# A hybrid decoder layer on one core: the scheduler's order taken from another timing model

## The chip, the cores and the metric

The kernel runs on one core of one Trainium2 chip. The metric is the device time of one execution in microseconds; three runs are timed, and one further execution is profiled.

## The reference

One layer of a decoder is computed for 2048 prompt tokens and for 64 sample tokens (8 sequences of 8), in fp32, with a model width of 1024. Two head groups share one input projection: attention over a sliding window of 128 with learned sinks, and an RWKV-7 recurrence whose state is corrected at each token. Their outputs are put side by side and projected; a gated feed-forward layer with a causal convolution of width 3 follows.

```python
proj = _rms_norm(x, g_pre_mix) @ w_in                 # q, k, v of attention and h of the recurrence
o_attn = attention(rope(q), rope(k), v, sinks)        # 8 heads of 64, 2 kv heads, window 128
def step(S, inp):                                     # the recurrence, 8 heads, S is 64 x 64
    r_t, w_t, k_t, v_t, kk_t, a_t = inp
    sa = jnp.einsum('bhij,bhj->bhi', S, kk_t)
    S = (S * w_t[:, :, None, :] - sa[..., None] * (kk_t * a_t)[:, :, None, :]
         + v_t[..., None] * k_t[:, :, None, :])
    return S, jnp.einsum('bhij,bhj->bhi', S, r_t)
o_rw = (group_norm(ys) + bonus) * g
mix = jnp.concatenate([o_attn, o_rw], axis=-1) @ w_out
x = x + _rms_norm(mix, g_post_mix)
z, u = split(_rms_norm(x, g_pre_ffn) @ w_ffn_in)      # 2 x 2816 columns
x = x + _rms_norm((silu(conv3(z)) * u) @ w_ffn_out, g_post_ffn)
```

## The kernel before

**Dense work.** The tokens are cut into five groups of 448 (the last holds 256 prompt and 64 sample tokens). For each group there are a projection P (20 tasks), an output projection O (8 tasks) and a feed-forward stage in two parts: F0, F2, F4, F6, F8 (60 tasks each) and F1, F3, F5, F7, F9 (6 tasks each). A task is one weight tile `w` of 128 x 1024. It is split into two rounded halves, `wh` by a cast on ACT (L351) and `wl` by a subtraction on DVE (L352), as the activations are (`xhi`, `xlo`), and gives 24 matmuls of 448 columns into one PSUM tile: `xhi`·`wh`, `xlo`·`wh` and `xhi`·`wl` for each of eight k. They show as `gm` or, in the second half of the feed-forward stage, as `pf`, at L182, the line of the helper that records every matmul. The stages follow one another in a list:

```python
order = [P[0], P[1], P[2], O[0], P[3], F[0], O[1], F[1], P[4], F[2], O[2], F[3],
         O[3], F[4], F[5], O[4], F[6], F[7], F[8], F[9]]
```

There are 11280 dense matmuls. P2 begins at the 960th, O0 at the 1440th, P3 at the 1632nd, F0 at the 2112th, P4 at the 3888th, O3 at the 6000th, F4 at the 6336th.

**The mixer.** The prompt is also cut into eight units of 256 tokens. A unit does two blocks of attention (`sc`, a softmax, the transposes `ppt`, then `po`) and the recurrence in four chunks of 64 tokens. The recurrence has a fixed chain of steps: the scores `sc_e` and `sc_o` from `ab`; from them a triangular system `G`; a trip through memory (`dgr`, then `gb`); its inversion by 31 steps of two DVE instructions each, every one on the result of the one ahead; a copy on ACT (L1045) and another trip through memory; small products `pz`; a chain over the chunks (`pc`, `pu`, `pS`); the group norm; and `finish`, with the transposes `pt`, the gate `pg` and the product `fin` (L1221), which goes to memory as `od`.

```python
v.tensor_tensor(out=tm, in0=col, in1=row, op=ALU.mult)                                   # L1041
v.tensor_tensor(out=tt[:nb, w:, 0:w], in0=tt[:nb, w:, 0:w], in1=tm, op=ALU.subtract)     # L1042
...
nc.scalar.copy(out=xx[:nb], in_=tt[:nb].rearrange("q s t -> q t s"))                     # L1045
```

An output projection reads `od` back (`r<-od`, then `xhi` and `xlo`) once the units under its tokens are done: O0 needs units 0 and 1, O1 units up to 3, O2 up to 5, O3 up to 6, O4 all of them. Its k from 0 to 3 are the attention half of the rows, k from 4 to 7 the recurrent half.

**What sets the order.** [...] First the program is written out as one sequence: while the dense stages run, `Flow` puts in the steps of a unit, by a clock that adds up estimated matmul times and by a window for each unit (unit 0 in P1, unit 1 in P2, unit 2 from P3 into F0, units 3 and 4 in F0, 5 and 6 in F2, 7 and the sample tokens in F4). [...] The order that comes out on each engine is fixed, and semaphores are set between the engines. On the chip an engine runs its instructions in that order, so an instruction that isn't ready holds up all that stand behind it on its engine. Nearly all DMAs are issued by SP.

## Time and profile before

| | |
|---|---|
| runs, us | 2903.93, 2908.86, 2918.96 (median 2908.86) |
| the profiled execution, us | 2909.42 |
| its span, us | 2907.6 |
| PE busy | 2772.0 us, 95% |
| DVE busy | 1925.0 us, 66% |
| ACT busy | 1409.1 us, 48% |
| POOL busy | 239.3 us, 8% |
| TensorE granted clock, mean | 0.97 |

The profiled execution took 1.8 us more than its span, and lies 0.6 us above the median. A share of busy time is a mean over stages. An interval of a view gives busy time by engine, and PEclk is the share of full speed that the throttle granted to TensorE.

### The profile page before, as it was taken

How to read it: one execution, taken by the hardware profiler on the slowest of the kernel's cores; microseconds unless marked ns; L12 is line 12 of the kernel's file. 1: busy time of each engine (PE TensorE's matmuls, PEld its weight loads, DVE VectorE, ACT ScalarE, POOL GpSimd, SP SyncE). 2: the span in 40 equal slices, each digit the busy share in tenths (PEclk: the TensorE clock that was granted, in tenths of full speed). 3: DMA queues.
4: the chain of work that ended last, by engine and by line, in shares of the span. 5: the costliest groups of instructions: out<-in, count | busy, mean ns of one | idle time of the engine just before them, and what ended most of it. 6: DMA issues, size and time to landing. Idle time of an engine off the chain costs nothing.

```text
span 2907.6 us, 46258 instructions
## 1 busy us (share of the span) xinstructions
PE 2772.0 (95%) x16993; PEld 2354.7 (81%) x16993; DVE 1925.0 (66%) x3792; ACT 1409.1 (48%) x2628; POOL 239.3 (8%) x519
## 2 busy tenths in 40 slices
PE   8997998989999999998999999899999999999997
PEld 6875776758778789776887898778989999999997
DVE  6884885686756655687665556965764764447666
ACT  6553545546564554454655434455333443334543
POOL 1010010010000000022000010000000001001111
PEclk9997999989999999998999999999999999999998
DMA  6665645746744343565544335664433553335443
GB/s 200 195 201 136 193 142 147 219 127 196 217 143 126 104 148 123 170 198 142 180 134 136 115 108 160 208 196 133 130 115 109 186 182 107 109 105 177 157 150 119
DMA packets 310529, 446.58 MB, mean 154 GB/s; under 512 B 118536, under 2 KB 238952, under 8 KB 310288
## 3 DMA queue, kind: packets, MB, share of 16 engines
q1 hardware_dynamic: 309872, 443.48, 49.5%
q8 instruction: 134, 2.20, 0.3%
q14 instruction: 91, 0.75, 0.1%
q10 hardware_dynamic: 432, 0.16, 0.0%
HBM read 362.19 MB, written 76.97 MB: 151 GB/s over the span
## 4 chain that ended last, share of the span: by engine, by line
PE 75%; DVE 13%; DMA 5%; ACT 3%; issue 3%; SPq 1%; DVEq 0%; ACTq 0%
PE gm L182 46%; PE pf L182 16%; PE pc L182 3%; DVE wl L352 2%; PE po L182 2%; DVE tt L1042 1%; DVE tmp L1041 1%; PE pz L182 1%; PE ppt L186 1%; ACT wh L351 1%; PE sc L182 1%; PE pu L182 1%; DMA w<-in_w_all 1%; PE pS L182 1%; PE sc_e L182 1%
## 5 line engine op out<-in xcount | busy, mean ns | idle before, releaser
L182 PE MATMUL gm<-xhi,wh 128*128 128x448 f32 (+3 forms) x2880 | 1056.1, 369 | 44.2 <-ACT wh L351 18.9
L182 PE MATMUL gm<-xhi,wl 128*128 128x448 f32 (+3 forms) x2880 | 1042.1, 363 | 14.9 <-DVE wl L352 14.6
L182 PE MATMUL gm<-xlo,wh 128*128 128x448 f32 (+3 forms) x2880 | 1039.5, 362 | 4.5 <-DVE xlo L352 4.2
L351 ACT CAST wh<-w 128x1024 fp32r<-128x1024 f32 (+1 forms) x470 | 489.5, 1042 | 720.3 <-PE gm L182 332.8
L352 DVE TENSOR_TENSOR wl<-w,wh 128x1024 fp32r<-128x1024 f32 (+1 forms) x470 | 569.9, 1213 | 381.8 <-ACT wh L351 377.6
L182 PEld LDWEIGHTS gm<-xhi,wh 128*128 128x128 f32 (+2 forms) x2880 | 544.2, 189 | 131.4 <-issue 31.4
L182 PEld LDWEIGHTS gm<-xhi,wl 128*128 128x128 f32 (+2 forms) x2880 | 544.3, 189 | 73.6 <-DVE wl L352 21.0
L182 PEld LDWEIGHTS gm<-xlo,wh 128*128 128x128 f32 (+2 forms) x2880 | 545.3, 189 | 60.3 <-DVE xlo L352 10.6
L182 PE MATMUL pf<-hh,wh 128*128 128x448 f32 (+1 forms) x880 | 317.8, 361 | 3.8 <-DVE acc L908 2.9
L182 PE MATMUL pf<-hl,wh 128*128 128x448 f32 (+1 forms) x880 | 312.5, 355 | 0.6 <-DVE hl L352 0.6
L182 PE MATMUL pf<-hh,wl 128*128 128x448 f32 (+1 forms) x880 | 312.4, 355 | 0.2 <-DVE wl L352 0.2
L881 POOL COPY zcar<-zz 128x2 f32<-128x2 f32 x110 | 74.4, 676 | 1547.6 <-ACT zz L870 1547.6
L908 DVE TENSOR_TENSOR acc<-acc,pf 128x448 f32<-128x448 f32 (+1 forms) x200 | 117.3, 589 | 103.4 <-PE pf L182 102.7
L182 PEld LDWEIGHTS pf<-hh,wh 128*128 128x128 f32 x880 | 165.3, 188 | 23.6 <-DVE acc L908 4.9
L182 PEld LDWEIGHTS pf<-hh,wl 128*128 128x128 f32 x880 | 165.3, 188 | 12.7 <-issue 1.0
L182 PEld LDWEIGHTS pf<-hl,wh 128*128 128x128 f32 x880 | 165.5, 188 | 11.8 <-DVE hl L352 1.0
L877 DVE SCALAR_TENSOR_TENSOR c<-zz,c_cw,c 128x448 f32<-128x448 f32 (+1 forms) x220 | 140.8, 640 | 26.2 <-ACT c L871 24.1
L891 DVE TENSOR_TENSOR c<-c,gm 128x448 f32<-128x448 f32 (+1 forms) x110 | 65.0, 591 | 120.4 <-PE gm L182 94.3
L884 ACT ACTIVATE c<-c 128x448 f32<-128x448 f32 (+1 forms) x110 | 61.2, 557 | 126.5 <-DVE c L877 89.3
L1041 DVE TENSOR_TENSOR tmp<-gb,tt 64x31 f32<-64x31 f32 (+21 forms) x279 | 91.4, 328 | 3.6 <-DMA gb<-dgr 1.0
L1042 DVE TENSOR_TENSOR tt<-tt,tmp 64x31 f32<-64x31 f32 (+21 forms) x279 | 91.9, 329 | 2.8
L351 ACT CAST xhi<-r 128x448 fp32r<-128x448 f32 (+1 forms) x112 | 59.3, 542 | 70.8 <-DMA r<-od 25.8
(272 smaller groups left out, 3115.6 us busy)
## 6 DMA issues: line engine op xcount, KB each, us to landing
w<-in_w SPq DMA_DIRECT2D x220, 512.0 KB
w<-in_w2q SPq DMA_DIRECT2D x100, 512.0 KB
w<-in_w_all SPq DMA_DIRECT2D x90, 512.0 KB
ab<-abd SPq DMA_DIRECT2D x66, 512.0 KB
w<-in_w_out SPq DMA_DIRECT2D x40, 512.0 KB
r<-in_xT SPq DMA_DIRECT2D x56, 224.0 KB
r<-od SPq DMA_DIRECT2D x32, 224.0 KB
x2d<-mx SPq DMA_DIRECT2D x32, 224.0 KB
```

The lines of the kernel that those rows point to most:

```text
L182: return self.te.matmul(out, lhsT, rhs, **kw)
L186: return self.te.transpose(*args)
L351: self.nc.scalar.copy(out=hi, in_=src)
L352: self.nc.vector.tensor_tensor(out=lo, in0=src, in1=hi.bitcast(F32), op=ALU.subtract)
L877: v.scalar_tensor_tensor(out=c[:, :npr], in0=z[:, j:j + npr], scalar=cw(j), in1=c[:, :npr], op0=ALU.mult, op1=ALU.add)
L881: nc.gpsimd.tensor_copy(out=sh.zcar[:, f, :], in_=z[:, npr:npr + 2])
L884: nc.scalar.activation(out=c, in_=c, func=AF.Silu)
L891: v.tensor_tensor(out=c, in0=c, in1=ps, op=ALU.mult)
L908: v.tensor_tensor(out=accs[c], in0=accs[c], in1=ps, op=ALU.add)
L1041: v.tensor_tensor(out=tm, in0=col, in1=row, op=ALU.mult)
L1042: v.tensor_tensor(out=tt[:nb, w:, 0:w], in0=tt[:nb, w:, 0:w], in1=tm, op=ALU.subtract)
```

## The change

The Tile context is opened with another argument: the scheduler's model of the machine is now its timeline model, where it was the clock of the instruction simulator. [...]

```diff
@@ -1652,7 +1652,7 @@
     a = {n: nc.dram_tensor("in_" + n, x.shape, mybir.dt.from_np(x.dtype), kind="ExternalInput").ap() for n, x in arrays.items()}
     for n, shape in out_shapes(seq).items():
         a[n] = nc.dram_tensor("out_" + n, shape, F32, kind="ExternalOutput").ap()
-    with tile.TileContext(nc) as tc:
+    with tile.TileContext(nc, schedule_with_timeline_sim=True) as tc:
         program(tc, nc, a, seq)
     r = run_bass_kernel_spmd(nc, [{"in_" + n: x for n, x in arrays.items()}], core_ids=[0]).results[0]
     return assemble({n: r["out_" + n] for n in out_shapes(seq)}, inputs, seq)
```

The two programs hold the same instructions but for the loads of ACT's function tables (28 before, 24 now); PE has 14441 matmuls in both. On PE an instruction stands on average 18 places from where the program wrote it before, and 131 now; on DVE 9 and 39, on ACT 31 and 45, on SP 16 and 29. The dense matmuls keep their order among themselves, nearly without exception, but the units stand elsewhere among them. The table counts the dense matmuls that stand ahead of a unit's first `sc_e`, first `pz` and last `pg` on PE.

| unit | before | now |
|---|---|---|
| 0 | 643, 848, 1039 | 646, 1082, 1440 |
| 1 | 1078, 1340, 1440 | 1440, 1440, 1476 |
| 2 | 1506, 1812, 2055 | 1479, 1857, 2273 |
| 3 | 2082, 2489, 2616 | 2309, 2719, 3171 |
| 4 | 2649, 2977, 3189 | 3217, 3624, 3925 |
| 5 | 3888, 4392, 4653 | 3953, 4594, 5031 |
| 6 | 4683, 5047, 5319 | 5068, 5479, 5907 |
| 7 | 5973, 6408, 6636 | 5988, 6348, 6718 |
| sample | 6783, 7045, 7181 | 6869, 7173, 7360 |

PE goes from a dense matmul to another kind 1020 times before and 748 times now; behind the start of O0 it is 759 and 609 times.

The first place is the end of P2 on PE. These rows of before run from the last dense matmuls of P2 over a product of its projection (`pb`) and the end of unit 1 (`pt`, `pg`) to two blocks' `sc` of unit 2 and the first matmuls of O0.

```order
L182 MATMUL gm<-xhi,wh 128x448
L182 MATMUL gm<-xlo,wh 128x448
L182 MATMUL gm<-xhi,wl 128x448
L182 MATMUL pb<-b_4964,c_blockones 128x448
L186 MATMUL pt<-c_ident,y 128x128
L182 MATMUL pg<-sg,c_g_up 128x256 x2
L186 MATMUL pt<-c_ident,y 128x128 x7
L182 MATMUL pg<-sg,c_g_up 128x256 x2
L182 MATMUL sc<-kx,q 128x256 x4
L182 MATMUL gm<-xhi,wh 128x448 x2
```

In the change P2's last dense matmul has behind it the end of unit 0 (`pt`, `pg`), and then unit 1 begins with the scores of its attention (`sc`) and of its recurrence (`sc_e`, `sc_o`); no dense matmul of P2 is left.

```order
L186 MATMUL pt<-c_ident,y 128x128 x7
L182 MATMUL pg<-sg,c_g_up 128x256 x2
L182 MATMUL sc<-kx,q 128x256 x4
L182 MATMUL sc_e<-ab 128x128 x4
L182 MATMUL sc_o<-ab 128x128 x4
L182 MATMUL sc<-kx,q 128x256 x4
L182 MATMUL sc_e<-ab 128x128 x4
L182 MATMUL sc_o<-ab 128x128 x4
L182 MATMUL sc_e<-ab 128x128 x4
L182 MATMUL sc_o<-ab 128x128 x4
L186 MATMUL ppt<-c_ident,s 128x128 x8
L182 MATMUL sc_e<-ab 128x128 x4
```

What moved is all of unit 1, from among P2's matmuls to behind them: between P2's last dense matmul and the 37th of O0 there now stand 359 matmuls of other kinds (183 ahead of O0's first, 176 behind its 36th). They are unit 0's end, the last products of P2's projection, and unit 1 from its first `sc` to its last `pg`. O0's 36 are three tasks' k from 0 to 3. On DVE the 62 steps of unit 1's inversion lie in the same place, behind P2's splits. The end of unit 1 in the change, with unit 2's first `sc` and O0's matmuls behind it, reads:

```order
L182 MATMUL pS<-uv,bkt 64x64 x7
L182 MATMUL pc<-uv,G 64x64 x4
L186 MATMUL pt<-c_ident,y 128x128
L182 MATMUL pg<-sg,c_g_up 128x256 x2
L186 MATMUL pt<-c_ident,y 128x128 x7
L182 MATMUL pg<-sg,c_g_up 128x256 x2
L182 MATMUL sc<-kx,q 128x256 x4
L182 MATMUL gm<-xhi,wh 128x448 x3
```

The second place is unit 0's inversion on ACT. In the rows of before, which lie in P1, the copy of its result (`gb<-tt`) stands right ahead of the cast of a weight tile (`wh`).

```order
L722 ACTIVATE e_2412<-L 128x7x64
L725 ACTIVATE e_2384<-L 128x448
L624 COPY qraw<-gm 128x448
L731 ACTIVATE tha<-tha,oka,hka 128x448
L1045 COPY gb<-tt 64x1024
L351 CAST wh<-w 128x1024
L1071 COPY zt<-pz 32x128 x2
```

In the change it stands ten casts of weight tiles later (45 are ahead of it where 35 were).

```order
L351 CAST wh<-w 128x1024
L639 COPY vts<-pvt 112x256 x2
L668 ACTIVATE hm<-gm,omu 128x448
L674 COPY h<-gm 128x448
L668 ACTIVATE hm<-gm,omu 128x448
L674 COPY h<-gm 128x448
L1045 COPY gb<-tt 64x1024
L555 ACTIVATE lo<-lo 32x448
L351 CAST wh<-w 128x8x96
```

What moved is the point in the stream of casts at which ACT takes up the inverse: it leaves P1, and unit 0's `pz` and chain go into P2 with it.

The third place is the start of F4 on PE, where unit 7's `pz` of before lie apart among dense matmuls and transposes (`ppt`) of the attention.

```order
L182 MATMUL pz<-zt,G 32x32
L186 MATMUL ppt<-c_ident,s 128x128 x3
L182 MATMUL pz<-zt,G 32x32 x7
L186 MATMUL ppt<-c_ident,s 128x128
L182 MATMUL gm<-xhi,wh 128x448
L182 MATMUL gm<-xlo,wh 128x448
```

In the change 48 of the 64 lie together behind 27 to 30 dense matmuls of F4.

```order
L182 MATMUL po<-pT,va 64x512
L182 MATMUL pz<-G,zt 32x32 x8
L182 MATMUL pz<-zt,G 32x32 x8
L182 MATMUL pz<-G,zt 32x32 x8
L186 MATMUL ppt<-c_ident,s 128x128 x4
L182 MATMUL pz<-zt,G 32x32 x8
L186 MATMUL ppt<-c_ident,s 128x128 x4
L182 MATMUL po<-pT,va 64x512
L182 MATMUL pz<-G,zt 32x32 x8
L182 MATMUL gm<-xhi,wh 128x448 x3
```

What moved is that the `pz` begin behind 12 dense matmuls of F4 where 72 stood ahead of them before, and come in a lump where they were spread over 42.

## Rows read from the trace of the kernel before

**Rows 1.** The page's head: span, and busy time of each engine.

```profile
span 2907.6 us, 46258 instructions
PE 2772.0 (95%) x16993; PEld 2354.7 (81%) x16993; DVE 1925.0 (66%) x3792; ACT 1409.1 (48%) x2628; POOL 239.3 (8%) x519
```

**Rows 2.** Busy time by interval: P1, P2, start of O0, P3, F0, P4, O3.

```profile
core 0: us, PE busy (x) PEld busy (x) DVE busy (x) ACT busy (x) POOL busy (x), PEclk, DMA share, GB/s
126.00:315.00 189.00, 169.40 (x1119) 128.16 (x1120) 127.97 (x268) 95.11 (x214) 11.79 (x38) 0.92 0.58 166
315.00:492.00 177.00, 169.45 (x1150) 126.86 (x1147) 131.93 (x283) 95.85 (x202) 18.38 (x39) 0.98 0.56 166
492.00:515.00 23.00, 13.23 (x28) 7.00 (x28) 14.17 (x45) 6.17 (x10) 0.07 (x1) 0.60 0.47 135
...
572.00:748.00 176.00, 160.96 (x1096) 124.83 (x1095) 138.93 (x304) 92.81 (x185) 15.37 (x36) 0.95 0.59 177
748.00:1149.00 401.00, 396.20 (x2680) 330.07 (x2679) 246.76 (x507) 206.43 (x388) 28.70 (x47) 1.00 0.44 135
...
1189.00:1247.00 58.00, 45.80 (x231) 37.74 (x229) 51.64 (x120) 26.13 (x64) 0.31 (x2) 0.92 0.62 196
...
1835.00:1891.00 56.00, 48.48 (x226) 40.62 (x224) 54.37 (x135) 27.32 (x58) 2.66 (x1) 0.91 0.64 203
```

**Rows 3.** Timeline of P1, PE and ACT: start, duration, and the idle time before.

```profile
234.01 0.36 PE L182 MATMUL gm<-xhi,wl 128*128 128x448 f32 x1
238.91 1.93 ACT L1045 COPY gb<-tt 64x1024 f32<-64x1024 f32 x1 [7.86 <-DVE tt L1042]
241.83 0.74 PE L182 MATMUL gm<-xhi,wh 128*128 128x448 f32 x1 [7.46 <-ACT wh L351]
```

**Rows 4.** Timeline of PE from P2's last dense matmul into O0.

```profile
491.64 0.36 PE L182 MATMUL gm<-xhi,wl 128*128 128x448 f32 x1
497.36 1.83 PE L182 MATMUL pb<-b,c_blockones 128*128 128x448 f32 x2 [5.36 <-DVE rsg L53]
...
506.77 2.08 PE L182 MATMUL pg<-sg,c_g_up 96*128 96x256 f32 x4 [0.40 <-DVE fin L1221]
...
513.63 1.11 PE L182 MATMUL gm<-xhi,wh 128*128 128x448 f32 x2
...
520.24 0.42 PE L182 MATMUL gm<-xhi,wh 128*128 128x448 f32 x1
```

**Rows 5.** Unit 4's steps, by tile: min/median/max ns, first and last start.

```profile
L182 PE MATMUL sc_e<-ab x32: 272/272/373, 912.0 to 938.3; 64*128 64x128 f32 x32
L1041 DVE TENSOR_TENSOR tmp<-gb,tt x31: 176/349/417, 948.7 to 987.4; 64x31 f32<-64x31 f32 x2, 64x60 f32<-64x60 f32 x2, 64x87 f32<-64x87 f32 x2, 64x112 f32<-64x112 f32 x2
L182 PE MATMUL pz<-zt,G x64: 191/191/212, 996.8 to 1013.8; 32*32 32x32 f32 x64
L182 PE MATMUL pu<-rhs,G x64: 218/218/268, 1021.3 to 1052.3; 64*64 64x64 f32 x64
L182 PE MATMUL pg<-sg,c_g_up x12: 377/378/380, 902.4 to 1074.3; 96*128 96x256 f32 x12
```

**Rows 6.** The chain that ended last: a stretch of dense matmuls alone.

```profile
2212.34 49.59 PE gm L182 x240
```

**Rows 7.** Timeline of PE in F0, at a switch to another kind and back.

```profile
1000.47 0.37 PE L182 MATMUL pf<-hl,wh 128*128 128x448 f32 x1
1000.77 0.43 PE L182 MATMUL pz<-zt,G 32*32 32x32 f32 x14
1001.13 0.48 PE L182 MATMUL pf<-hh,wl 128*128 128x448 f32 x1
1001.45 0.37 PE L182 MATMUL pf<-hh,wh 128*128 128x448 f32 x1
```

**Rows 8.** F4's first dense matmul in the timeline, and unit 7's products by tile.

```profile
1890.56 0.57 PE L182 MATMUL gm<-xhi,wh 128*128 128x448 f32 x2
L182 PE MATMUL pz<-zt,G x64: 191/191/212, 1908.9 to 1925.6; 32*32 32x32 f32 x64
```

## The prediction

> **What bounds the kernel now.** I read the page's head first. PE is busy for 2772.0 of 2907.6 us, so 135.6 us are idle, and DVE as the next engine has 66% [rows 1]. The kernel is bound by PE, and a new order can win only in three ways: it fills PE's idle time, it keeps the clock up, or it saves time between matmuls. It can lose without such a limit, since each engine's order is fixed.
>
> The intervals say where the idle time is [rows 2]. P1 and P2 (126 to 492 us) have 366 us of which PE is busy for 169.40 + 169.45, so 27.2 us are idle, and the clock is 0.92 and 0.98. The 23 us behind P2 hold 13.23 us of work at a clock of 0.60. P3 (572 to 748) has 15.0 us idle at 0.95. F0 with two whole units in it has 4.8 us idle in 401 at 1.00. The two stages behind it that begin while a unit inverts, P4 and O3, have 12.2 and 7.5 us idle. Where there is much dense work around a unit, the unit costs PE no waiting; where there is little, it does.
>
> What a wait looks like is seen in P1 [rows 3]. PE ends a dense matmul at 234.4 us and takes the next at 241.8: it waits for a cast of a weight tile, which stands on ACT behind the copy of unit 0's inverse, and that copy waited 7.86 us for DVE's last step. At the end of P2, 28.6 us lie between the last dense matmul's start at 491.64 and the first of O0 that needs the recurrent half of the mixer's output, the thirteenth, at 520.24 [rows 4].
>
> Two prices are needed. A dense matmul alone takes 49.59/240 = 0.206 us [rows 6]. A unit costs PE about 50 us of its time: F0's interval has 396.2 us of PE work, 1440 x 0.206 = 296.6 of it dense, and the rest is that of two units [rows 2, 6]. How long a unit takes from its scores to its last gate is read at unit 4, in the middle of F0: 912.0 to 1074.3, 162.3 us [rows 5]. The unit is a chain far longer than its work, and it is free only as long as dense matmuls stand beside it.
>
> **The change part by part.** No instruction is taken out that would count: four table loads of ACT, which has half its time free, are costed at nothing. Everything is in the order.
>
> *Unit 1 behind P2.* The order has 359 matmuls of other kinds between P2's last dense one and the 37th of O0, with only 36 dense ones among them. So unit 1's chain stands bare: PE can't take another task before the last `pg` has its operands. I build its length from unit 4's steps [rows 5]. Scores: 26.3 us there with dense matmuls between them; 20 here, from 64 x 0.272 = 17.4 and the attention's `sc`. From the last score to the inversion: 10.4. The inversion: 38.7 there; with nothing between, 31 x 2 x 0.349 = 21.6, and since the unit's own attention uses DVE in the same place I take 31, a little above the middle. From there to the first `pz`: 9.4. Products and chain: 55.5 (996.8 to 1052.3), 54 without dense matmuls in the way. Group norm and end: 22.0. That is 146.8, with 126 and 162 as ends (the lower has scores at 17.4, the inversion at 21.6 and 45 for products and chain).
>
> Ahead of it PE has unit 0's end and P2's last products: before, the same kinds of work took from 491.64 to the end of the last `pg` at 508.8, and I take 18. Behind it the result goes to memory, is read back and split, as before from 508.2 to 520.2: 12. So 177 us stand where 28.6 stood. O0's 24 more dense matmuls that now lie inside take 5 us off: **+143**. The ends are +120 (unit 126, 18 and 10 around it) and +166 (unit 162, 18 and 12, and 8 more for the part of PE's work that would run at the 0.60 of rows 2).
>
> *P1 and P2 without unit 1.* They lose its 50 us of work. They also lose waits: at most the 27.2 us idle and some 12 us that the lower clock cost outside of the idle time (0.08 x 189 + 0.02 x 177 = 18.7 in all). Unit 0 stays there, now with P1 and P2 around it, and the copy that held up a cast [rows 3] has ten casts more ahead of it. I take 28 of the 39. Some 3 us come from fewer switches. **-80**, with -60 and -92 as ends (10 of the 39, or all of it and no switch left that costs).
>
> *P3 and later.* The 15 us idle in P3 [rows 2] may shrink since unit 2's inversion now falls behind 1812 + 45 dense matmuls, later by two tasks, and its chain moves into F0: **-8**, between 0 and -15. For P4 with its 12.2 us, a unit's chain stands elsewhere: **-4**, between 0 and -12.
>
> *Switches.* Behind the start of O0 PE changes from dense to other matmuls 609 times and not 759. At such a switch two dense matmuls stand 0.30 and 0.32 us before the next start, and not 0.206: 1000.47 to 1000.77, and 1001.13 to 1001.45 [rows 6, 7]. So a switch there and back costs 0.2 us, half of it each way, and 150 x 0.2 counts a there and back for each one saved: 30. That price comes from one place where the small products came at once, and most of what follows larger tiles will have cost less, so I take half: **-15**, between 0 and -30. [...]
>
> *Unit 7 at F4's start.* Before, its `pz` came at 1908.9 with F4 begun at 1890.56 [rows 8], 18.3 us later and behind 72 dense matmuls. The change wants the first behind 12 and 48 of 64 behind 30, that is 2.5 to 6.2 us into F4. If the chain to them is no earlier than before, PE stands for about 12 to 16 us; but other waits of O3 (7.5 us, rows 2) would be in that same time, and its inversion may begin sooner with unit 6's end out of the way. **+5**, between 0 and +16.
>
> Sum: 143 - 80 - 8 - 4 - 15 + 5 = +41. From the profiled execution's 2909.42 us, 0.6 above the median, that gives **2950 us**.
>
> **The rivals.** The first ends on the other side: *the bare chain is short and the rest wins*. Its place is the same gap behind P2. If unit 1's inversion runs beside unit 0's end (they use DVE and PE) and its attention fills the waits, the gap is near its lower end of 154; then 154 - 28.6 - 5 = +120, against -92, -15, -12, -30 with nothing lost at F4: -29, or 2880; with switches at 15 it is -14, or 2895. It decides from a gap of about 136 us with my other terms. For it speaks that DVE steps of 0.349 would allow 21.6; against it that unit 4's steps don't sum to under 126 even with each at its shortest. I give 2890 and a chance of 0.13.
>
> The second: *new waits elsewhere*. An instruction stands on average 131 places from where it was written on PE, and ACT's and DVE's orders moved less, so a lump may meet operands that are late; unit 7's, at the full +16, is the one with a row, and the units 3 to 6, up to 736 dense matmuls later than before at their end, may meet the stage that needs them (O1 needs unit 3, whose last `pg` now stands 381 ahead of O1's first dense matmul at 3552, so 78 us ahead; O3 needs unit 6, 93 ahead of 6000, 19 us). The lump at the clock of 0.60 [rows 2] would be 8 to 20 more. Together 2975 to 3000, chance 0.2. [...]
>
> The third: *no net effect*. The gap is near its lower end, 155 and so +121, and P1 and P2 give back all they can, -92; with -22 from the other terms that is +7, or 2916. Chance 0.17.
>
> **How the numbers follow.** My sum has 0.5, its upper rival 0.2, no change 0.17, and faster 0.13. Half a per cent, 14.5 us, is about what a measurement of this kernel can tell from none. Slower by more holds my own case and the second rival: 0.70. Range: the lower end is the cheap gap with the full relief, just under the 2895 above: 2893. The upper end has the long gap, +166, with the smallest relief, -60, and -22 for the rest: +84, 2993; 17 us of new waits, the size of unit 7's, make it 3010.
>
> **What would show it.** After P2's last dense matmul PE should show a stretch of about 175 us with little work, a low clock, waits for DVE at the inversion and for memory around it. P1 and P2 should be some 80 us shorter, without the 7 us wait ahead of a cast. F0 and F2 should keep their clock of 1.00 and lose a few us. A wait of some us for `pz` should stand behind F4's first dense matmuls. I am wrong if the gap is under 135 us, if P1 and P2 gave back under 60, or if the difference lies in a stage behind F0.

## The result and the profile after

The changed kernel takes 3011.52 us, median of four runs (2997.72 to 3020.44), against 2907.12 (2903.93 to 2918.96) before: a ratio of 1.0342, with an interval from 1.0322 to 1.0361. It is slower, as forecast, but by 104 us where 41 were forecast, and 1.5 us above the stated range. Its profiled execution has a span of 3010.1 us.

The head of the changed kernel's page, which answers to [rows 1], shows that PE's idle time grew from 135.6 to 205.4 us and its busy time by 32.7, with the same number of matmuls.

```profile
span 3010.1 us, 46327 instructions
PE 2804.7 (93%) x16993; PEld 2412.9 (80%) x16993; DVE 1942.2 (65%) x3792; ACT 1403.6 (47%) x2624; POOL 267.0 (9%) x519
```

Where the time went is read from the start of each stage's first dense matmul in the two traces.

| stage begins | before | after | behind |
|---|---|---|---|
| P1 | 126.7 | 132.5 | 5.8 |
| P2 | 315.2 | 283.4 | -31.7 |
| end of P2's last dense matmul | 492.0 | 419.6 | -72.4 |
| O0's 37th | 526.4 | 582.0 | 55.6 |
| P3 | 572.0 | 630.3 | 58.3 |
| F0 | 748.1 | 793.1 | 45.0 |
| O1 | 1149.2 | 1173.7 | 24.6 |
| P4 | 1247.4 | 1297.2 | 49.8 |
| F2 | 1350.7 | 1407.2 | 56.5 |
| O3 | 1835.1 | 1895.2 | 60.1 |
| F4 | 1890.6 | 1970.2 | 79.6 |
| O4 | 2291.2 | 2371.0 | 79.7 |
| F6 | 2322.0 | 2409.5 | 87.5 |
| F8 | 2651.5 | 2744.1 | 92.7 |
| end of the span | 2907.6 | 3010.1 | 102.5 |

There are two losses: 58 us up to P3, and 42 from O3 on. Between P3 and O3 the two kernels take nearly the same time, 1263.1 and 1264.9 us, though all the units there stand elsewhere. The intervals of the changed kernel, cut at its own stages (P1, P2, the gap behind P2, P3, F0, O1 with F1, P4, O3, F6, F8), answer to [rows 2]. The second cut is at 422.0, where the last product of P2's projection ahead of a long wait ends, 2.4 us behind P2's last dense matmul. In [rows 2] the row from 1189 to 1247 is F1; P4 begins where it ends.

```profile
132.50:283.40 150.90, 136.25 (x650) 107.11 (x650) 118.62 (x241) 74.00 (x160) 17.87 (x38) 0.95 0.63 181
283.40:422.00 138.60, 135.41 (x990) 110.87 (x990) 94.65 (x163) 78.02 (x147) 9.38 (x36) 0.98 0.62 180
422.00:582.00 160.00, 108.05 (x694) 77.07 (x694) 73.66 (x202) 45.90 (x123) 2.13 (x3) 0.59 0.29 84
630.30:793.10 162.80, 146.46 (x966) 116.54 (x965) 122.42 (x253) 84.31 (x168) 20.05 (x34) 0.95 0.60 183
793.10:1173.70 380.60, 378.38 (x2304) 322.67 (x2303) 248.65 (x498) 185.21 (x339) 29.38 (x49) 1.00 0.41 128
1173.70:1297.20 123.50, 106.94 (x855) 89.21 (x854) 75.87 (x178) 65.42 (x141) 0.94 (x2) 0.91 0.54 170
1297.20:1407.20 110.00, 108.07 (x637) 92.68 (x638) 92.92 (x212) 58.59 (x135) 36.95 (x64) 0.97 0.64 195
1895.20:1970.20 75.00, 49.69 (x232) 42.51 (x231) 65.05 (x169) 31.20 (x62) 1.97 (x1) 0.84 0.53 174
...
2409.50:2714.90 305.40, 299.91 (x1453) 275.16 (x1454) 162.28 (x233) 120.43 (x175) 27.04 (x43) 0.98 0.39 126
2744.10:2967.20 223.10, 215.08 (x1452) 214.43 (x1452) 142.94 (x248) 104.55 (x179) 35.25 (x86) 0.98 0.48 156
```

The third row is the first loss: 160 us with a granted clock of 0.59 (a share of full speed) and 52 us idle. The last two rows hold no unit at all, and yet F6 and F8 lost 5.1 and 7.7 us: PE was idle there for 5.5 and 8.0 us at a clock of 0.98. Before, in the same two stages, it was idle for 0.7 and 1.3 us at a clock of 1.00.

```profile
2322.00:2622.30 300.30, 299.58 (x1461) 271.88 (x1462) 164.28 (x241) 122.47 (x178) 25.83 (x43) 1.00 0.40 128
2651.50:2866.90 215.40, 214.13 (x1452) 212.30 (x1451) 142.06 (x248) 102.54 (x179) 36.54 (x86) 1.00 0.50 161
```

**The gap behind P2.** Unit 1's steps by tile in the changed kernel (min, median and max ns, then first and last start) answer to [rows 5]. Two rows go by tile name and hold a few steps of a neighbour: of the `sc_e` the last 7, from 583.4, are unit 2's, and of the `pg` the first 4, at 436.8, are unit 0's.

```profile
L182 PE MATMUL sc_e<-ab x39: 417/418/580, 441.6 to 584.8; 64*128 64x128 f32 x39
L1041 DVE TENSOR_TENSOR tmp<-gb,tt x31: 183/349/417, 469.9 to 499.4; 64x31 f32<-64x31 f32 x2, 64x60 f32<-64x60 f32 x2, 64x87 f32<-64x87 f32 x2, 64x112 f32<-64x112 f32 x2
L182 PE MATMUL pz<-zt,G x64: 229/236/258, 505.0 to 520.2; 32*32 32x32 f32 x64
L182 PE MATMUL pu<-rhs,G x64: 218/267/365, 536.4 to 562.8; 64*64 64x64 f32 x64
L182 PE MATMUL pg<-sg,c_g_up x12: 417/634/793, 436.8 to 577.7; 96*128 96x256 f32 x12
```

The waits of PE in this stretch (us in all, times, the longest) name the same chain.

```profile
PE pz L182 <- DMA zt<-dtr: 21.9, 2, 21.5
PE pb L182 <- DVE b L741: 7.2, 1, 7.2
PE ppt L186 <- DVE s L1241: 5.7, 1, 5.7
PE pt L186 <- DVE y L1194: 5.3, 2, 4.9
```

The unit runs through from about 439 to the end of its last product at 579.7 us, 140 us in all (438.8 to 579.7, `sc` of its attention to `pg`), with nothing dense beside it but O0's 36. The inversion's 31 steps take 29.5 us, 469.9 to 499.4.

**From O3 on.** The timeline at F4's start, DVE and then PE, shows the largest of the late waits. DVE does eight gains (L939) and eight sums (L941) of F3, the feed-forward stage that ended before O3, and the last of the sums wait for their reloads; the sums of O3's squares (L769) stand between them. PE's order has the norm's first product (`ms`), which needs the last of those sums, straight behind O3's last dense matmul, and PE stands for 14.08 us. In these 14 us DVE is busy for 11.1, of which the gains and sums of F3 take 5.9 and L769 takes 4.3; only 3.0 are idle time ahead of sums that wait for reloads.

```profile
1950.37 4.25 DVE L939 SCALAR_TENSOR_TENSOR acc<-acc,c_gT,rb 128x448 f32<-128x448 f32 x7
1954.54 0.61 DVE L769 TENSOR_TENSOR sa<-sa,sq 128x448 f32<-128x448 f32 x1
...
1964.25 0.63 DVE L941 TENSOR_TENSOR acc<-acc,r 128x448 f32<-128x448 f32 x1 [1.63 <-DMA r<-x2d]
1964.79 0.62 DVE L769 TENSOR_TENSOR sa<-sa,sq 128x448 f32<-128x448 f32 x1
...
1967.25 0.62 DVE L769 TENSOR_TENSOR sa<-sa,sq 128x448 f32<-128x448 f32 x1
1967.92 1.65 PE L182 MATMUL ms<-c_ones,sa 128*112 128x1 f32 x8 [14.08 <-DVE sa L769]
```

In the order before, 22 of F4's dense matmuls stood ahead of that product, and now none; at F6's start it is 9 and none. Before, the product came 5.7 us into F4 and waited for nothing:

```profile
1896.29 0.85 PE L182 MATMUL ms<-c_ones,sa 128*112 128x1 f32 x8
```

The place alone doesn't make the wait. For the norm ahead of P4 the change puts the same product behind F1's last dense matmul too, where 21 of F1's were still to come before, and there it waits 0.7 us. What differs is what DVE still has in line at that moment: there the last sum of squares starts at 1269.24 us, just as F1's last dense matmul ends, and at F4's start it starts at 1967.25, 13.4 us behind O3's.

The wait in F8 is of another kind: PE waits 8.0 us for `c` (L891), a step of F8 itself that stands on DVE behind F7's sums.

```profile
PE gm L182 <- DVE c L891: 8.0, 1, 8.0
```

### The profile page after: what moved, and what is told of

Same layout as the page of the kernel before. It is cut to its first block, busy times and chain, and to the rows that moved or that the text cites. A ratio compares the mean times of both kernels' runs of the same rounds, so it can differ in the third digit from the quotient of the medians.

```text
span 3010.1 us, 46327 instructions
## 1 busy us (share of the span) xinstructions
PE 2804.7 (93%) x16993; PEld 2412.9 (80%) x16993; DVE 1942.2 (65%) x3792; ACT 1403.6 (47%) x2624; POOL 267.0 (9%) x519
## 4 chain that ended last, share of the span: by engine, by line
PE 80%; DVE 8%; DMA 7%; ACT 3%; issue 1%; SPq 1%; POOL 0%; ACTq 0%; DVEq 0%
PE gm L182 50%; PE pf L182 16%; PE pc L182 2%; PE po L182 2%; PE sc L182 1%; DVE wl L352 1%; DMA r<-xnd 1%; PE ppt L186 1%; DMA r<-in_xT 1%; PE sc_e L182 1%; DVE tmp L1041 1%; DVE tt L1042 1%; PE pz L182 1%; PE pu L182 1%; DMA r<-x2d 1%
## 5 line engine op out<-in xcount | busy, mean ns | idle before, releaser
L182 PE MATMUL gm<-xhi,wh 128*128 128x448 f32 (+3 forms) x2880 | 1045.4, 367 | 71.8 <-DVE c L891 15.9
L182 PEld LDWEIGHTS gm<-xhi,wl 128*128 128x128 f32 (+2 forms) x2880 | 547.9, 190 | 55.6 <-issue 8.9
L881 POOL COPY zcar<-zz 128x2 f32<-128x2 f32 x110 | 82.1, 747 | 1454.3 <-ACT zz L870 1454.3
L891 DVE TENSOR_TENSOR c<-c,gm 128x448 f32<-128x448 f32 (+1 forms) x110 | 65.0, 591 | 96.7 <-PE gm L182 92.5
L351 ACT CAST xhi<-r 128x448 fp32r<-128x448 f32 (+1 forms) x112 | 59.1, 543 | 102.1 <-DMA r<-xnd 35.8
L352 DVE TENSOR_TENSOR xlo<-r,xhi 128x448 fp32r<-128x448 f32 (+1 forms) x112 | 64.1, 590 | 62.3 <-ACT xhi L351 61.9
```

The source lines that it names most:

```text
L182: return self.te.matmul(out, lhsT, rhs, **kw)
L351: self.nc.scalar.copy(out=hi, in_=src)
L352: self.nc.vector.tensor_tensor(out=lo, in0=src, in1=hi.bitcast(F32), op=ALU.subtract)
L881: nc.gpsimd.tensor_copy(out=sh.zcar[:, f, :], in_=z[:, npr:npr + 2])
L891: v.tensor_tensor(out=c, in0=c, in1=ps, op=ALU.mult)
```

## The experiments

**How the orders were set.** The first runs give every engine an order that is written out (`order` holds the positions of the instructions as the program wrote them). Each instruction is tied (`NoSync`) behind the one that is to stand ahead of it on its engine.

```diff
+    ins = [i for i in nc.cur_bb.bb.instructions if type(i).__name__ != "BassTilePoolBoundary"]
+    how = mybir.DependencyInfo(mybir.DependencyClass.NoSync, mybir.DependencyReason.DATA)
+    last = {}
+    for p in order:
+        i = ins[p]
+        if i.engine in last:
+            tc.add_manual_dep(i, last[i.engine], how, reason="order")
+        last[i.engine] = i.name
```

At the first dense matmul of P3 (the 1632nd), and again at the 6000th, the two orders have done nearly the same work: 9 and 15 instructions of the 22926 lie on the other side of the cut. So either order can be taken up to a cut and the other behind it. The 6000th is F3's first dense matmul, not O3's as I had it ahead of the prediction and in the expectations; O3 begins at the 6144th. All runs that are cut "at O3" are cut at the 6000th. F3 takes 44.7 us before and 45.0 after, so the readings hold.

**e1, the head changed.** 

> The changed order on every engine up to the first dense matmul of P3 (the 1632nd), the order of before from there. Theory 1, each place pays for itself: the changed kernel had lost 58.3 us when P3 began, so 2907 + 58 = 2965. Rival, the loss behind P3 follows from the lump (units late, buffers late): with the lump left in, the later stages lose their 42 us too, so about 3005.

Measured: 2964.23 against 2910.62 us, 1.0189 (1.0174 to 1.0205), +54.

**e2, the rest changed.** 

> The order of before up to P3's first dense matmul, the changed order from there. Theory 1: 2907 + 100.3 - 58.3 = 2949. Rival, knock-on from the lump: without the lump the later order costs nothing, 2907, or gains the 15 us that fewer switches were costed at, 2892.

Measured: 2952.12 us, 1.0151 (1.0135 to 1.0166), +42.

**e3, the middle changed.** 

> The changed order only between P3's first dense matmul and O3's first (the 6000th), where units 2 to 6 lie; the order of before ahead and behind. Theory 1: the changed kernel was 58.3 us behind at the start of the stretch and 60.1 at its end, so +2, 2909. Rival, the moved units gain there by fewer switches and the lump's clock hides it: 2892 to 2900.

Measured: 2911.74 us, 1.0002 (0.9993 to 1.0012).

**e4, changed from F3 on.** 

> The order of before up to O3's first dense matmul, the changed order from there (unit 7, the sample tokens, O3, F4 to F9). Theory 1: +40.2, the 19.5 of O3 and some 20 behind it, 2947. Rival, knock-on: 2907.

Measured: 2952.96 us, 1.0157 (1.0140 to 1.0174), +42.

The four say the same: each place pays for itself. The head's 54 and the 42 behind the second cut make 96 of the 104 (of 101, if the changed kernel is set against the 2910.62 of before that was measured beside these runs), and the moved units between them cost and give nothing. Knock-on from the lump has fallen, and so has a gain by fewer switches: from P3 to O2 PE leaves its dense matmuls 218 times and not 272, and e3 is no faster.

**e8, unit 1's inversion left out.** The changed order, with

```diff
+            if u == 1 and j:
+                continue
             m, w = 31 - j, j + 1
```

> The changed order on every engine, with 30 of the 31 steps of unit 1's inversion left out (60 DVE instructions; unit 1's part of the output is not the reference's). The loop took from 469.8 to 499 us in the changed kernel. Theory 1, the gap behind P2 is one chain over the engines: 25 to 30 us shorter, so 2982 to 2987. Rival, the gap is set by PE's work at the half clock: less than 5, 3006 or more.

Measured: 2992.18 us, 1.0280 (1.0264 to 1.0295), 19 us less than the changed kernel; in the traces P3 begins 20.0 us earlier. The gap is the unit's chain and not PE's work, but the run fell short of the 25 to 30 us that were expected. Of the loop's 29.5 us some 10 aren't given back: the first `pz` comes at 486 and not 505. The copy of the inverse stands on ACT behind the softmax of the unit's attention, which the fixed order keeps, and starts at 480.4.

**e11, matmuls added to hold the clock.** In the changed order, ahead of unit 1's last transposes of its attention,

```diff
+        if u == 1:
+            ps = self.ps("fill")
+            for _ in range(80):
+                te.te.matmul(ps[:, 0:128], self.sh.ident, self.sh.ones, start=True, stop=True)
```

> The changed order, with 80 matmuls of 128x128 added on PE (their result is used nowhere) between unit 1's attention and its first pz, where PE stood idle for 21.5 us at half clock. Theory 3, the low clock makes the bare chain behind it longer: products and chain run faster, 10 to 15 us off the gap, 2997 to 3003. Rival, the chain is set by copies, DVE and memory, or the clock falls again at once: no change, 3008 to 3014, or longer by what the added matmuls delay.

Measured: 3012.60 us, 1.0342 (1.0323 to 1.0361), as the changed kernel. The intervals of this run are cut ahead of, at and behind the added matmuls; below them stand the changed kernel's for the last two.

```profile
424.00:470.00 46.00, 35.57 (x119) 24.92 (x119) 27.08 (x64) 11.84 (x34) 2.19 (x3) 0.52 0.43 117
470.00:505.00 35.00, 24.23 (x185) 20.76 (x184) 27.32 (x86) 7.33 (x21) 0.00 (x0) 0.89 0.14 38
505.00:582.00 77.00, 61.59 (x554) 45.69 (x555) 20.80 (x54) 27.25 (x68) 0.00 (x0) 0.66 0.31 94
```

```profile
470.00:505.00 35.00, 6.30 (x21) 2.50 (x22) 27.24 (x86) 7.33 (x21) 0.00 (x0) 0.58 0.15 39
505.00:582.00 77.00, 64.39 (x551) 48.96 (x551) 19.19 (x52) 26.60 (x68) 0.00 (x0) 0.63 0.28 84
```

The added matmuls brought the clock from 0.58 to 0.89 where they stood, and it was at 0.66 behind them, 0.63 without. Cut at what PE did, the rows are sharper. Over the added matmuls and the end of the attention the clock was 1.00. Then PE waited 10.78 us for the inverse's way through memory, and over the first products behind that wait the clock was 0.50.

```profile
506.51 0.28 PE L182 MATMUL pz<-zt,G 32*32 32x32 f32 x2 [10.78 <-DMA zt<-dtr]
470.00:495.70 25.70, 24.20 (x185) 20.76 (x184) 22.30 (x69) 5.41 (x20) 0.00 (x0) 1.00 0.12 37
506.50:531.20 24.70, 21.77 (x178) 14.00 (x179) 1.79 (x3) 9.64 (x27) 0.00 (x0) 0.50 0.39 112
```

So one of the two conditions of the rival came true: the clock had fallen again when the products ran, from 1.00 ahead of the stand-still of 10.78 us to 0.50 behind it. The run doesn't show what products and chain would take at full clock; that stays open.

**e6 and e7, P3 ahead of O0.** The list of stages is changed, once with the timeline model and once with the old one.

```diff
-        order = [P[0], P[1], P[2], O[0], P[3], F[0], O[1], F[1], P[4], F[2], O[2], F[3], O[3], F[4], F[5], O[4], F[6], F[7], F[8], F[9]]
+        order = [P[0], P[1], P[2], P[3], O[0], P[4], F[0], O[1], F[1], F[2], O[2], F[3], O[3], F[4], F[5], O[4], F[6], F[7], F[8], F[9]]
```

> The list of stages is P0, P1, P2, P3, O0, P4, F0, O1, F1, F2 and on as before, and the scheduler uses the timeline model as in the change. Here unit 1's scores and inversion lie among P3's matmuls and 241 others stand in a lump ahead of O0's 37th, from unit 1's first pz on. Theory 1, the head's loss is what of unit 1's chain stands bare: its last 75 of 160 us stay, so the head loses some 27 instead of 54, and the later 42 stay: 65 to 75 us over the same list under the old model. Rival, any such list loses as much, 97 over it.

> The same list of stages under the old model, to stand beside the run with the timeline model. Theory 1: P3's 480 dense matmuls cover the end of unit 1, so the 28.6 us between P2's last matmul and O0's recurrent half and the 15 idle us of P3 shrink: 2880 to 2900. Rival: the end of unit 1 only moves to O0's new place and the cost with it, 2905 to 2915.

Measured: 2961.01 us with the timeline model, 1.0169 (1.0152 to 1.0186), and 2896.21 with the old one, 0.9947 (0.9933 to 0.9962). The model costs 65 us with this list and 104 with the other, so 39 less where P3's matmuls stand beside unit 1's scores and inversion. Theory 1 holds for both, in the first at the lower end of its 65 to 75 us. In the traces the run with the timeline model is 1.5 us behind the other when P4 begins, 20 at F0's start, 28 at O3's and 73 at the end: the loss at the head has shrunk from 58 us to 20, and some 45 from O3 on have stayed. Under the old model the list beats both kernels, the one before by 0.5%.

**e14, and unit 5 behind F1.** e7 with

```diff
-                    (f(F[0], 0.53), f(F[0], 0.93)), (f(F[2], 0), f(F[2], 0.47)), (f(F[2], 0.47), f(F[2], 0.93)), (f(F[4], 0), f(F[4], 0.5))]
+                    (f(F[0], 0.53), f(F[0], 0.93)), (f(F[2], 0.15), f(F[2], 0.55)), (f(F[2], 0.55), f(F[2], 0.95)), (f(F[4], 0), f(F[4], 0.5))]
```

> The list of stages P0, P1, P2, P3, O0, P4, F0, O1, F1, F2 under the old model, with unit 5's window put from F2's start to 15% of F2 (and its end, and unit 6's window, by 8%). In the run that measured 2896 PE waited 19 us in F1 and at F2's start for DVE, whose line held unit 5's inversion and attention. Theory: those waits go, 2880 to 2886. Rival: unit 5 then presses on unit 6 and O3, and nothing is gained, 2893 to 2900.

Measured: 2885.83 us, 0.9923 (0.9909 to 0.9937), the fastest kernel of the study that computes everything. The intervals over the end of F1 and the start of F2, of e7 and then of e14, show the waits gone: PE was idle for 23.6 of 44 us, and is for 4.1 of 50.

```profile
1296.00:1340.00 44.00, 20.40 (x71) 15.13 (x71) 43.22 (x124) 15.79 (x36) 0.18 (x1) 0.69 0.40 131
```

```profile
1290.00:1340.00 50.00, 45.95 (x221) 37.47 (x220) 46.42 (x108) 27.30 (x55) 3.61 (x7) 0.90 0.63 205
```

**e5, the ends of the stages paced as before.** From the second cut on the order is the changed one, but the steps of the stages' ends are put back by position among the dense matmuls.

> As the run with the changed order from O3 on, except that the ends of the stages (squares, norm, gain and sum with the residual, on DVE, ACT, PE and SP, of O3 and O4 and of F3, F5, F7, F9) stand where the order of before has them; unit 7, the sample tokens and all dense work stay in the changed order. Theory 2, the late 42 us are DVE's and SP's: the gain-and-sum steps of a finished stage (L939, L941), which wait for their reloads, stand in a lump ahead of what the next stage needs: 30 of the 34 us of waits go, and the clock they cost, so 2915, at most 2920. Rival, the lump of unit 7's products and the shifted unit: 2945 or more.

Measured: 3009.72 us, 1.0338 (1.0322 to 1.0353). The merged order made waits of its own: O3 took 92.7 us and F4 397.5, against 76.6 and 367.4 in e4. It says nothing on theory 2, only how little such an order bears.

**e9 and e10, the sums on GpSimd.** The order of e4, and that of before as the control, with

```diff
-                v.tensor_tensor(out=accs[c], in0=accs[c], in1=x, op=ALU.add)
+                nc.gpsimd.tensor_tensor(out=accs[c], in0=accs[c], in1=x, op=ALU.add)
```

> The changed order from O3's first dense matmul on, as in the run that measured 2953, with one step on another engine: the 40 sums of a finished stage with its reloaded residual (L941) run on GpSimd in the same place of the order, so that DVE no longer waits for those reloads. Theory 2, DVE's line behind those waits makes PE's late waits (14 us at F4's start, 3 and 5 at F6's, 8 in F8): 15 to 20 us less, 2933 to 2938. Rival, the waits come from the norm's products on PE and the order of SP's loads: 2948 or more.

> The order of before on every engine, with the same 40 sums on GpSimd, as the control of the run above. Both theories: within 0.3% of before, 2905 to 2918, since DVE isn't what PE waits for in F1 to F9 there.

Measured: 2965.12 us, 1.0182 (1.0158 to 1.0207), and the control 2925.27, 1.0039 (1.0023 to 1.0054). Theory 2 missed its 2933 to 2938, and the control missed its 2905 to 2918. The sums on GpSimd cost some 10 us in the changed order (53 us above before where e4 is 42 above) and 13 in the other, and the distance between the orders stays at 40. The run lies in the rival's open range of 2948 or more, but the timeline of e9 at F4's start shows why it can't tell: while GpSimd does its sums, a step of the inversion that takes 0.20 us in e4 (the last row) takes 1.14.

```profile
1895.33 12.27 POOL L941 TENSOR_TENSOR acc<-acc,r 128x448 f32<-128x448 f32 x4 [72.16 <-DVE acc L939]
1903.33 1.14 DVE L1041 TENSOR_TENSOR tmp<-gb,tt 64x60 f32<-64x60 f32 x1
```

```profile
1901.28 0.20 DVE L1041 TENSOR_TENSOR tmp<-gb,tt 64x60 f32<-64x60 f32 x1
```

**e12 and e13, gain, reload and sum left out.** The order of e4, and that of before as the control, with

```diff
             for c in range(KT):
-                x = take(c)
-                v.scalar_tensor_tensor(out=accs[c], in0=accs[c], scalar=sh.gT[:, 2 * KT + c:2 * KT + c + 1], in1=st["r"],
-                                       op0=ALU.mult, op1=ALU.mult)
-                v.tensor_tensor(out=accs[c], in0=accs[c], in1=x, op=ALU.add)
                 self.store(a["y"][c, :, t0:t0 + n], accs[c])
```

> The changed order from O3 on, as in the run that measured 2953, with the last step of the five F stages left out: the gain (L939), the reload of the residual and the sum (L941), so that the output y is the bare product; 80 DVE instructions and 40 DMAs fewer, everything else in its place. Theory 2, those steps stand in a lump on DVE and SP ahead of what the next stage needs: of the 34 us of PE's waits behind O3 20 to 25 go, with some clock, 2923 to 2933. Rival, unit 7's lump, the norm's products and PE's own order make them: 2945 or more.

> The order of before with the same steps left out, the control. Both theories: nothing that PE waits for but the end of the kernel, where the last sums stand bare: 2903 to 2910, a few us less than before.

Measured: 2923.07 us, 1.0053 (1.0037 to 1.0069), and the control 2886.75, 0.9929 (0.9914 to 0.9944). PE's waits from O3 on, of e4 and then of e12, fell: for the squares (`sa`) from 18.4 to 7.7 us, for `c` from 12.7 to 9.0, for `xhi` from 6.7 to 3.2.

```profile
PE ms L182 <- DVE sa L769: 18.4, 3, 13.7
PE gm L182 <- DVE c L891: 12.7, 3, 8.1
PE gm L182 <- ACT xhi L351: 6.7, 4, 4.9
PE ms L182 <- DVE dg L783: 5.3, 2, 3.0
PE gm L182 <- ACT mx L819: 5.3, 1, 5.3
```

```profile
PE gm L182 <- DVE c L891: 9.0, 4, 4.0
PE ms L182 <- DVE sa L769: 7.7, 2, 6.1
PE gm L182 <- ACT mx L819: 5.7, 1, 5.7
PE gm L182 <- ACT xhi L351: 3.2, 3, 1.6
```

By itself e12 meets theory 2. But the control, expected at 2903 to 2910, got faster by 22 us too, 11 of them at the very end of the kernel, so the distance between the orders only went from 42 to 36. The gains and sums make a part of the late waits; as their whole cause theory 2 has fallen.

**e15 and e16, PE's order tied and the others left free.** Up to the second cut the order of before. From there PE's order is tied to one of the two, and DVE, ACT, SP and POOL are left to the scheduler with the other model.

> The order of before on every engine up to O3; from there PE keeps the order of before, and the other engines are left to the scheduler with the timeline model. Theory 4, PE's own order makes the late waits, since it puts the norm's products straight behind a stage's last matmul and the other engines' orders follow PE's: 2907 to 2915. Rival, the lines of DVE, ACT and SP make them: 2935 to 2950.

> The order of before on every engine up to O3; from there PE keeps the changed order, and the other engines are left to the scheduler with the old model. Theory 4: 2940 to 2955, as with the changed order on every engine (2953). Rival: 2907 to 2920.

Measured: 2955.18 us with PE as before and the others by the timeline model, 1.0146 (1.0123 to 1.0169); 2951.51 with PE as changed and the others by the old one, 1.0134 (1.0112 to 1.0155). The second lies in theory 4's range, the first above both ranges, and the losses beside their own runs of before are 39.5 and 35.8 us.

The two runs did not cross the engines as they were meant to: DVE's order came out nearer to the one that goes with PE's. In e16 DVE's instructions stand on average 2.3 places from where e4 has them and 9.2 from where before has them, behind the cut; so e16 is nearly e4 again and can't tell PE's order from the others'. In e15 it is 7.7 from e4 and 4.7 from before. The waits of PE from O3 on, of e15 and then of e16, lie in different places.

```profile
PE ms L182 <- DVE sa L769: 9.1, 4, 5.9
PE gm L182 <- DVE c L891: 6.2, 3, 4.8
```

```profile
PE ms L182 <- DVE sa L769: 21.7, 3, 13.7
PE gm L182 <- ACT xhi L351: 6.5, 1, 6.5
PE gm L182 <- DVE c L891: 1.2, 1, 1.2
```

In e16, as in e4, the 13.7 us at F4's start and the waits at F6's start stay. The wait for `c` in F8 goes from 8.1 to 1.2 under the same order of PE, so it belongs to the others' lines. With PE's order of before the waits at F4's and F6's start are gone or small, and yet nothing is won: F3 takes 59.0 us, F4 381.7, F6 308.2 and F8 220.2, where before they took 44.7, 371.2, 300.2 and 215.4. So the late 42 us are shown by place, and it is shown that PE's order of before does not by itself avoid them. Which engine's order makes them, and what an order would have to keep between the engines to lose nothing, stays open.

## Why the prediction was right, and where it was wrong

**Unit 1 behind P2, +143: right, a little large.** From the end of P2's last dense matmul to O0's 37th it was 162.4 us, and 34.4 before (28.6 to O0's thirteenth, [rows 4]): +128. Of my terms, unit 0's end with P2's last products took 19 (18), the unit 140 (147), and the way of its result to O0 2 us and not 12, since PE takes O0's next matmul at 582.0, right behind the last product, which ends at 579.7.

**P1 and P2, -80: right in the sum.** From P1's start to the end of P2's last dense matmul the time went from 365.3 to 287.1 us, -78.2. The make-up was another: PE's busy time fell by 68.8 (338.85 to 270.02), where I had taken 50 for the unit's work, and its idle time only by 10.2, from 27.2 to 17.0, where I had taken 28 for idle time and clock together. That the sum came out so near is in part luck. The 7.46 us ahead of a cast [rows 3] are gone. P0, which I had left alone, lost 5.8. The net was +55.6 at O0's 37th matmul and +58.3 at P3's start, for +63.

**P3, P4 and the switches, -27: wrong.** P3 did become 13.3 us shorter and F0 20.4, but O1 with F1 took 25.3 more, P4 6.7, and F2, O2 and F3 3.6. The work of units 2 to 4 had moved down the kernel and was done there; from P3 to O3 nothing was gained (+1.8, and 1.0002 in e3). A price read at one switch, times a count of switches, was no saving. The count was wrong too: 1020 and 748, 759 and 609 count the changes in both directions, so 75 times there and back were saved behind O0's start and not 150, which by my price is 15 us and 7.5 at the half. And the 12.2 us that I gave to P4 are F1's [rows 2]: P4 was idle for 8.0 us before and for 1.9 after, and still took 6.7 more; F1's idle time grew from 12.6 to 16.3.

**Unit 7 at F4's start, +5: the place was right, the cause and the size were not.** O3 with this wait took 75.0 us and not 55.5. PE stood for no more than 0.8 us at unit 7's `pz`, which began 5.2 us into F4, where before it was 18.3 [rows 8]. What it waited for were the squares of O3's norm: that a wait stands at the place I named is luck.

**The step that failed** is the one that isn't there. I followed the units through the order and took the ends of the stages (norms, gains, sums, reloads) as they were, since the dense matmuls kept their order: their term was nothing, without a reason from any row. Part by part the traces' 102.5 us, where I had 41, come out so: the head +58.3 for +63, P3 to O3 +1.8 for -27, and from O3 on +42.4 for the +5 of unit 7. So the -27 were wrong by 29 us, and the missing term by 37. The 42 lie in O3 (19.5), O4 (7.8) and F6 to F9 (some 15, where no unit stands), and the waits read there are at the ends of stages. The second rival, new waits elsewhere at 2975 to 3000, comes nearest, though the time lies above it; but I had placed the waits at O1 and O3 for units 3 and 6, and at neither was a unit late. Unit 6 also had more room than I gave it, since O3 begins 237 dense matmuls behind its last `pg` and not 93. DVE's mean displacement of 39 places, which the change showed, was never read at the stages' ends. Of my signs of being wrong one came true: the loss beyond the forecast lies in stages behind F0.

The rival that ends faster had its condition, a gap under 136 us, and the gap was 162. What a unit costs that stands bare is seen at the head: e1 costs 54 us for one, and e7, where P3's matmuls stand beside the unit's end, is 14.4 us faster than before (2896.21 against 2910.62). That fewer switches raise the clock is shown by no run here: F0 had a clock of 1.00 both with 98 switches and with 63, so it could show no more, and the stretch of e3 with its fewer switches took the same time.

## What to carry to other kernels

Where a scheduler's order changes, read it at every place where a stage ends, on every engine that has work between the stages, and not only where the largest blocks moved: here a product that was put straight behind the last matmul of a stage made PE wait for what DVE still had in line, 14.1 us at F4's start and 0.7 ahead of P4. The price of a long chain that loses the independent matmuls beside it can be summed step by step from a place where it is covered (147 us summed, 140 measured). Cutting between two orders in time, at a place where both have done the same work, told more than moving single steps or giving the engines different orders: steps moved by position made new waits (e5: 92.7 us for O3 and not 76.6), and with PE's order fixed DVE's came out near to the one that went with it (e16: 2.3 places from it on average).

## What the runs showed that was not expected

Some of DVE's steps stretch while GpSimd adds tiles of 128x448: 1.14 us instead of 0.20 for the same 64x60 step in e9, and 10 to 13 us over the kernel for 40 such sums. And the order of before, which has little idle time in F5 to F8, still gained 22 us when the gains, reloads and sums were left out: 11.3 at the end of the kernel (19.6 to 8.3 us behind the last dense matmul's start), 4.5 in O3, and the rest in pieces of 1 to 3 us.
